# Gate and up products of sixteen experts: the high and low halves of the tokens as one moving operand of 512 columns

## The chip, the core and the metric

The kernel runs on one core of a Trainium2 chip. The time is device microseconds of one execution, from start to end. A profiled execution also leaves a trace: when each instruction ran on TensorE (PE), VectorE (DVE), ScalarE (ACT), GpSimd (POOL) and in the DMA queues, and what ended each idle stretch.

## The reference

One layer: a mixer, and then a mixture of experts that choose their tokens. The change lies in the experts. Each of 16 experts takes the 256 tokens that score highest for it, out of 2048.

```
aff = softmax(h @ w_router + b_router)                 # 2048 x 16
gate, idx = top_k(aff.T, 256)                          # per expert
xe = h[idx]                                            # 16 x 256 x 1024
hid = silu(xe @ w_gate) * (xe @ w_up)                  # 1024 -> 1024, per expert
ye = (hid @ w_down) * gate                             # 1024 -> 1024
out = rms_norm(h_lat + gt2 * scatter_add(idx, ye)) * final_norm_g
```

All of it is fp32. The kernel keeps that precision by splitting every matrix operand into a high part, which TensorE's fp32r format holds, and a low part, the rest. A product is then three matmuls: high by high, high by low and low by high.

## The kernel before

The experts run one after the other, in `moe`. The list below follows one of them, number e.

**Weights.** An expert has six chunks of 1024 x 512: gate and up for the first 512 hidden columns, gate and up for the second 512, and two of the down matrix. They are called gate 0, up 0, gate 1, up 1, down 0 and down 1 here. Each comes in two halves of 256 columns (a and b). For a half, `load_w` issues a DMA of 1 MB into `raw` (2 buffers), ACT casts it to the high part `wh` (L183) and DVE subtracts to get the low part `wl` (L184). That subtraction frees the `raw` buffer for the next DMA. There are three buffers for whole chunks, so a chunk's cast waits until TensorE has finished the chunk three places before it.

**Tokens.** `route(e)` turns the scores into token numbers: 16 compares on DVE (`oh`, L1334), 32 small matmuls (L1339), and a reduction on DVE that writes `idx` (L1343). `idx` has two buffers. `expert_in(e)` then gathers 256 rows of `f_rows` with two indirect DMAs from POOL's queue (`xg`, L1364), turns them with 16 TensorE transposes (`xt`, L1372), and splits them into `xS` (ACT L1374, DVE L1375). For most experts this is done for expert e+1 while expert e is in its first half.

**Gate and up.** Eight tiles of 128 hidden columns, called f0 to f7 here. A tile of `ps_a` (PSUM, three buffers, name `gu`) holds gate and up sums, 2 x 256 tokens. Each is 8 x 3 matmuls of 256 columns by `mm3` (L194 to L196). ACT takes the SiLU out of PSUM (L1392), DVE multiplies with the up half out of PSUM (L1393), and ACT and DVE split the result into `hS` (L1395, L1396).

**Down.** 96 matmuls of 512 columns (`dn`, the same L194 to L196) in four groups; DVE scales each group into `ye` (L1412). When both groups of one half of the tokens are there, POOL issues an indirect DMA that adds 128 rows of `ye` to `h_rows` (L1449). It reads the token numbers in `idx`. The second half's DMA waits for the first half's. The last three experts read the rows and write them back in place of adding, and `final_tile` does the last norm for the rest, beside experts 13 and 14.

**What sets the order.** The instructions of each engine stand in one fixed order, which a scheduler chose when the program was built, by a timeline of its own. It may put instructions of two experts side by side. On each engine they run in that order.

**Buffers that bind.** `idx` of expert e+1 takes the buffer of expert e-1, and so it can only be written when the gathers and the adding DMAs of expert e-1, which read that buffer, have landed. `xS` has one buffer, so the split for e+1 waits for the last gate and up matmul of e.

Of the kernel before, what the change touches and what calls it, by code (L numbers as in the profile page):

```python
# [7 lines left out]
F32 = mybir.dt.float32  # L8
F32R = mybir.dt.float32r
# [3 lines left out]
AF = mybir.ActivationFunctionType  # L13
OP = mybir.AluOpType
AX = mybir.AxisListType
PS = bass.MemoryType.PSUM
DR = bass.MemoryType.DRAM

P = 128
D = 1024  # L20
KT = 8
# [1183 lines left out]
def moe(tc, ctx, env):  # L1205
    nc = tc.nc
# [5 lines left out]
    with ExitStack() as pd:  # L1212
# [2 lines left out]
            raw_f = pf.enter_context(tc.tile_pool(name="rawF", bufs=2, side="right"))  # L1215
            pre = [load_w(raw_f, wr, w[0, 0, :, 0:512], nc.gpsimd, parts=PP, cast=C1) for w in (w_gate, w_up)]
        rt = pd.enter_context(tc.tile_pool(name="rtD", bufs=1))
        ps_a = pd.enter_context(tc.tile_pool(name="psaD", bufs=3, space=PS))
        ps_d = pd.enter_context(tc.tile_pool(name="psdD", bufs=2, space=PS))
        ps_t = pd.enter_context(tc.tile_pool(name="pstD", bufs=2, space=PS))  # L1220
        ps_c = pd.enter_context(tc.tile_pool(name="pscD", bufs=1, space=PS))

        tk = ExitStack()
        wk = tk.enter_context(tc.tile_pool(name="wkT", bufs=1))
        vp = ps_c.tile([P, 2, P], F32, name="c")
        for s in range(2):
            nc.tensor.transpose(vp[:, s, :], AFF[:, s].rearrange("p e g -> p (e g)"), ident)
        blkb, belb, cand, step, cK, siob = topc
# [8 lines left out]
        X = nhi  # L1237
        cd = cand[:, 0, :]
        for i in range(15):
            tp = ps_c.tile([P, 512], F32, name="c")  # L1240
            nc.tensor.matmul(tp[:, 0:3], blkb, cK, start=True, stop=False)
            cn = wk.tile([P, 2], BF, name="cn", bufs=15)
            for j in range(2):
                jk = wk.tile([P, 256], BF, name=f"jk{j}", bufs=1)
                cj = nc.vector.tensor_scalar(jk, X, cd[:, j:j + 1], None, op0=OP.is_le, op1=OP.add,
                                             accum_out=cn[:, j:j + 1])
            if i == VI:
                after_first = cj
            ca = wk.tile([P, 1], BF, name="ca", bufs=15)
            jk = wk.tile([P, 256], BF, name="jk2", bufs=1)  # L1250
            with nc.allow_low_precision(reason="whole numbers up to 256 are exact"):
                nc.scalar.activation(jk, X, AF.Sign, scale=-1.0, bias=cd[:, 2:3], accum_out=ca)
            nc.tensor.matmul(tp[:, 0:2], blkb, cn, start=False, stop=False)
            nc.tensor.matmul(tp[:, 2:3], blkb, ca, start=False, stop=True)
            if i not in (6, 14):
                tcd = wk.tile([P, 4], F32, name="tcd", bufs=15)
                nc.vector.tensor_tensor(tcd, cand[:, i + 1, :], cd[:, 3:4].to_broadcast([P, 4]), op=OP.add)
            if i == 14:
                lob = wk.tile([P, 1], F32, name="lob", bufs=1)
                nc.vector.tensor_scalar(lob, cd[:, 3:4], -1.0, float(LO0), op0=OP.mult, op1=OP.add)  # L1260
            ge = wk.tile([P, 3], F32, name="ge", bufs=15)
            inc = wk.tile([P, 1], F32, name="inc", bufs=15)
            nc.vector.scalar_tensor_tensor(ge, tp[:, 0:3], CAP - 0.5, step[:, i:i + 1].to_broadcast([P, 3]),
                                           op0=OP.is_ge, op1=OP.mult, accum_out=inc)
            if i == 6:
                npre = wk.tile([P, 1], F32, name="npre", bufs=1)
                nc.vector.tensor_tensor(npre, cd[:, 3:4], inc, op=OP.subtract)
                t1 = wk.tile([P, 256], U16, name="t1", bufs=1)
                t2 = wk.tile([P, 256], U16, name="t2", bufs=1)
                nc.vector.scalar_tensor_tensor(t1, nhi, npre, nlow, op0=OP.is_equal, op1=OP.mult)  # L1270
                nc.vector.tensor_scalar(t2, nhi, npre, float(LO0), op0=OP.is_gt, op1=OP.mult)
                nc.vector.tensor_tensor(t1, t1, t2, op=OP.max)
                X = t1
                cd = cand[:, 7, :]
                hb = wk.tile([P, 1], I32, name="hb", bufs=1)
                nc.vector.tensor_scalar(hb, npre, -65536.0, 65536.0 * HI0, op0=OP.mult, op1=OP.add)
            elif i < 14:
                cd = wk.tile([P, 4], F32, name="cd", bufs=15)
                nc.vector.tensor_tensor(cd, tcd, inc.to_broadcast([P, 4]), op=OP.subtract)
# [7 lines left out]
        eq = wk.tile([P, 256], BF, name="eq", bufs=1)  # L1287
        nc.vector.tensor_scalar(gt, V, thr, None, op0=OP.is_gt, op1=OP.add, accum_out=ct[:, 0:1])
        nc.vector.tensor_scalar(eq, V, thr, None, op0=OP.is_equal, op1=OP.add, accum_out=ct[:, 1:2])
        tp = ps_c.tile([P, 512], F32, name="c")  # L1290
        nc.tensor.matmul(tp[:, 0:2], belb, ct, start=True, stop=True)
        nc.tensor.matmul(tp[:, 2:3], blkb, ct[:, 0:1], start=True, stop=True)
        off = wk.tile([P, 3], F32, name="off", bufs=1)
# [11 lines left out]
        nc.vector.scalar_tensor_tensor(se, se, off[:, 1:2], eq, op0=OP.add, op1=OP.mult)  # L1305
        nc.vector.scalar_tensor_tensor(sg, sg, BIG, se, op0=OP.add, op1=OP.add)
        SL = rt.tile([P, 2, NE, 8], F32, name="SL", bufs=1)
        sp = ps_c.tile([P, 2, P], F32, name="c")
        for s in range(2):
            nc.tensor.transpose(sp[:, s, :], sg[:, s * P:(s + 1) * P], ident)  # L1310
        nc.vector.tensor_copy(SL.rearrange("p s e g -> p s (e g)"), sp)
# [16 lines left out]
        wk = pd.enter_context(tc.tile_pool(name="wkD", bufs=1))  # L1328

        def route(e):  # L1330
            oh = ohp.tile([P, 2, 8, 256], BF, name="oh", bufs=1)
            for s in range(2):
                for g in range(8):
                    nc.vector.tensor_scalar(oh[:, s, g, :], siob, SL[:, s, e, g:g + 1], None, op0=OP.is_equal)  # L1334
            rp = ps_c.tile([P, 2, 256], F32, name="c")
            for hf in range(2):
                for i in range(16):
                    s, g = divmod(i, 8)
                    nc.tensor.matmul(rp[:, hf, 0:5], oh[:, s, g, hf * P:(hf + 1) * P], vals[:, s, e, g, :],  # L1339
                                     start=(i == 0), stop=(i == 15))  # L1340
            idx = rt.tile([P, 2], I32, name="idx", bufs=2)
            with nc.allow_low_precision(reason="token numbers are whole"):
                nc.vector.tensor_reduce(idx, rp[:, :, 0:2], axis=AX.X, op=OP.add)  # L1343
            rs = rt.tile([P, 2, 5], F32, name="rs", bufs=2)
            nc.vector.tensor_copy(rs, rp[:, :, 0:5])
            gate = rt.tile([P, 2], F32, name="gate", bufs=2)
            nc.vector.tensor_tensor(gate, rs[:, :, 2], rs[:, :, 3], op=OP.add)
            nc.vector.tensor_tensor(gate, gate, rs[:, :, 4], op=OP.add)
            return idx, gate
# [10 lines left out]
        def expert_in(e):  # L1360
            idx, gate = route(e)
            xg = wk.tile([P, 2, D], F32, name="xg", bufs=1)
            for hf in range(2):
                last[1] = nc.gpsimd.indirect_dma_start(out=xg[:, hf, :], out_offset=None, in_=f_rows,  # L1364
                                                       in_offset=bass.IndirectOffsetOnAxis(ap=idx[:, hf:hf + 1], axis=0))
            xS = [wk.tile([P, KT, 256], F32R, name=f"xS{s}", bufs=1) for s in range(2)]
            for kk in range(4):
                ps = ps_t.tile([P, 2, 256], F32, name="xt")
                for k2 in range(2):
                    for hf in range(2):  # L1370
                        k = 2 * kk + k2
                        nc.tensor.transpose(ps[:, k2, hf * P:(hf + 1) * P], xg[:, hf, k * P:(k + 1) * P], ident)  # L1372
                ks = slice(2 * kk, 2 * kk + 2)
                nc.scalar.activation(xS[0][:, ks, :], ps, AF.Copy)  # L1374
                last[0] = nc.vector.tensor_tensor(xS[1][:, ks, :], ps, xS[0][:, ks, :].bitcast(F32), op=OP.subtract)  # L1375
            return idx, gate, xS

        def expert(e, st, mid=None):
# [3 lines left out]
            for i in range(2):  # L1382
                gw = next_w(w_gate[0, e, :, i * 512:(i + 1) * 512])
                uw = next_w(w_up[0, e, :, i * 512:(i + 1) * 512])
                for f in range(4):
                    fs = slice(f * P, (f + 1) * P)
                    pg = ps_a.tile([P, 2, 256], F32, name="gu")
                    for j, w in enumerate((gw, uw)):
                        for k in range(KT):
                            mm3(pg[:, j, :], w[0][:, k, fs], w[1][:, k, fs], xS[0][:, k, :], xS[1][:, k, :], k, KT)  # L1390
                    sg_ = wk.tile([P, 256], F32, name="sgl", bufs=2)
                    nc.scalar.activation(sg_, pg[:, 0, :], AF.Silu)  # L1392
                    nc.vector.tensor_tensor(sg_, sg_, pg[:, 1, :], op=OP.mult)  # L1393
                    ff = 4 * i + f
                    nc.scalar.activation(hS[0][:, ff, :], sg_, AF.Copy)  # L1395
                    nc.vector.tensor_tensor(hS[1][:, ff, :], sg_, hS[0][:, ff, :].bitcast(F32), op=OP.subtract)  # L1396
                if mid is not None and i == 0:
                    nx = mid()
# [195 lines left out]
```

## Time and profile before

| What | Value |
|---|---|
| Median of 3 runs | 2503.82 us (2495.16 to 2510.73) |
| Profiled execution: its time, its span | 2509.17 us, 2507.4 us |
| PE busy | 2360.6 us, 94% of the span |
| DVE, ACT, POOL busy | 1594.8, 1114.9, 526.2 us |
| Mean granted TensorE clock | 0.968 of full speed |
| DMA moved | 528.97 MB, mean 211 GB/s |

A busy PE is not PE at its peak: the records of its matmuls overlap, so the pace is read from the distance between their starts. The engines other than PE are idle for a good part, and that costs nothing unless somebody waits.

### The profile page before, as it was taken

To read this page: it belongs to the slowest core of one execution; us is meant where nothing else is said; L and a number is where in the kernel's file an instruction comes from. 1 tells how busy PE (TensorE), PEld (TensorE's weight loads), DVE (VectorE), ACT (ScalarE), POOL (GpSimd) and SP (SyncE) were. 2 spreads that over 40 slices of the span, in tenths; PEclk is the share of its full clock that TensorE was granted. 3 is DMA by queue.
4 is the path that set the end of the run, shared out by engine and by line. 5 is a ranking of instruction groups with operands and counts; after the bars stand their busy time and mean duration, and the time that the engine had idled before them with its cause. 6 is when DMAs were issued, how large, how long until landed. Compare 5 with 4: busy or idle time off the path is not lost.

```text
span 2507.4 us, 43163 instructions
## 1 busy us (share of the span) xinstructions
PE 2360.6 (94%) x16841; PEld 2159.0 (86%) x16841; DVE 1594.8 (64%) x3337; ACT 1114.9 (44%) x2002; POOL 526.2 (21%) x420
## 2 busy tenths in 40 slices
PE   7999999998889999999937999999999999999997
PEld 4999999887768898888826999999999999998897
DVE  6688665468778465676674556555565565556674
ACT  4554555576623443343322444444444444444553
POOL 2321222211022633232252011111111011011211
PEclk9999999999988999999967999999999999999999
DMA  8676654499946997565353676666766766668894
GB/s 260 199 231 206 208 171 161 141 298 304 281 128 187 264 274 227 192 197 175 139 168 110 190 230 202 195 200 211 219 212 190 220 210 199 205 208 270 304 309 145
DMA packets 473056, 528.97 MB, mean 211 GB/s; under 512 B 104500, under 2 KB 392061, under 8 KB 470803
## 3 DMA queue, kind: packets, MB, share of 16 engines
q1 hardware_dynamic: 455298, 465.63, 58.3%
q0 software_dynamic: 17120, 59.77, 8.3%
q8 instruction: 133, 2.18, 0.4%
q10 hardware_dynamic: 432, 0.79, 0.1%
q14 instruction: 73, 0.59, 0.1%
HBM read 400.45 MB, written 125.67 MB: 210 GB/s over the span
## 4 chain that ended last, share of the span: by engine, by line
PE 59%; DMA 12%; issue 6%; DVE 5%; ACT 3%; POOL 2%; SPq 0%; POOLq 0%; DVEq 0%; ACTq 0%
PE gu L195 6%; PE gu L196 6%; PE gu L194 6%; DMA xg<-f_rows,idx 4%; PE dn L195 4%; PE dn L194 4%; PE dn L196 4%; PE uv L194 2%; PE uv L196 2%; PE uv L195 2%; PE mx L194 2%; PE mx L196 2%; PE mx L195 2%; ACT wh L183 2%; PE ks L1005 1%
## 5 line engine op out<-in xcount | busy, mean ns | idle before, releaser
L184 DVE TENSOR_TENSOR wl<-raw,wh 128x2048 fp32r<-128x2048 f32 (+1 forms) x212 | 445.8, 2114 | 306.2 <-ACT wh L183 306.1
L194 PE MATMUL gu<-xS,wh 128*128 128x256 f32 x2048 | 580.6, 285 | 3.7 <-ACT wh L183 3.5
L196 PE MATMUL gu<-xS,wl 128*128 128x256 f32 x2048 | 578.6, 285 | 4.8 <-DVE wl L184 4.8
L195 PE MATMUL gu<-xS,wh 128*128 128x256 f32 x2048 | 580.3, 284 | 0.0
L183 ACT ACTIVATE wh<-raw 128x2048 fp32r<-128x2048 f32 (+1 forms) x218 | 381.5, 1771 | 372.2 <-DMA raw<-in_w_gate_dram 146.4
L194 PEld LDWEIGHTS gu<-xS,wh 128*128 128x128 f32 x2048 | 393.5, 192 | 5.9 <-ACT wh L183 4.2
L196 PEld LDWEIGHTS gu<-xS,wl 128*128 128x128 f32 x2048 | 391.8, 192 | 6.8 <-DVE wl L184 5.7
L195 PEld LDWEIGHTS gu<-xS,wh 128*128 128x128 f32 x2048 | 393.6, 192 | 1.1
L194 PE MATMUL pj<-aS,wh 128*128 128x258 f32 x832 | 238.2, 290 | 2.3 <-DVE y L460 2.3
L195 PE MATMUL pj<-aS,wh 128*128 128x258 f32 x832 | 238.3, 288 | 0.2 <-DVE aS L358 0.2
L196 PE MATMUL pj<-aS,wl 128*128 128x258 f32 x832 | 237.6, 287 | 0.6 <-DVE wl L184 0.6
L195 PE MATMUL dn<-wl,hS 128*128 128x512 f32 (+1 forms) x520 | 201.9, 389 | 1.8 <-DVE wl L184 1.8
L194 PE MATMUL dn<-wh,hS 128*128 128x512 f32 (+1 forms) x520 | 203.5, 391 | 0.0
L1449 POOL DMA_INDIRECT h_rows<-ye,idx x26 | 66.5, 2558 | 644.4 <-DVE ye L1412 551.7
L196 PE MATMUL dn<-wh,hS 128*128 128x512 f32 (+1 forms) x520 | 200.9, 387 | 0.0
L194 PEld LDWEIGHTS pj<-aS,wh 128*128 128x128 f32 x832 | 157.1, 190 | 3.6 <-issue 2.0
L195 PEld LDWEIGHTS pj<-aS,wh 128*128 128x128 f32 x832 | 158.6, 191 | 0.6 <-DVE aS L358 0.4
L196 PEld LDWEIGHTS pj<-aS,wl 128*128 128x128 f32 x832 | 157.9, 190 | 1.0 <-DVE wl L184 0.8
L194 PE MATMUL uv<-wh,ast 128*128 128x512 f32 x384 | 155.1, 404 | 0.0
L196 PE MATMUL uv<-wh,ast 128*128 128x512 f32 x384 | 151.7, 395 | 0.0
L195 PE MATMUL uv<-wl,ast 128*128 128x512 f32 x384 | 151.5, 395 | 0.0
L1395 ACT ACTIVATE hS<-sgl 128x256 fp32r<-128x256 f32 x128 | 53.0, 414 | 180.2 <-DVE sgl L1393 180.1
(479 smaller groups left out, 4583.8 us busy)
## 6 DMA issues: line engine op xcount, KB each, us to landing
raw<-in_w_gate_dram SPq DMA_DIRECT2D x64, 1024.0 KB
raw<-in_w_up_dram SPq DMA_DIRECT2D x64, 1024.0 KB
raw<-in_w_down_dram SPq DMA_DIRECT2D x64, 1024.0 KB
kv<-kv SPq DMA_DIRECT2D x140, 256.0 KB
raw<-in_w_mod_dram SPq DMA_DIRECT2D x18, 1024.0 KB
a_sp<-aS SPq DMA_DIRECT2D x32, 512.0 KB
ast<-a_sp POOLq DMA_DIRECT2D x16, 1024.0 KB, 7.6
raw<-in_w_in_dram SPq DMA_DIRECT2D x12, 1024.0 KB
```

Source lines behind the costliest of these rows:

```text
L183: nc.scalar.activation(wh[:, ks, s:s + 256], raw[:, ks], AF.Copy)
L184: (lo_eng or nc.vector).tensor_tensor(wl[:, ks, s:s + 256], raw[:, ks], wh[:, ks, s:s + 256].bitcast(F32), op=OP.subtract)
L194: pace(nc.tensor.matmul(ps, ah, bh, start=(k == 0), stop=False), after)
L195: nc.tensor.matmul(ps, ah, bl, start=False, stop=False)
L196: return nc.tensor.matmul(ps, al, bh, start=False, stop=(k == nk - 1))
L1005: nc.tensor.matmul(sp[:, h, :], kr[:, h, :], vn[:, h, :], start=True, stop=True)
L1395: nc.scalar.activation(hS[0][:, ff, :], sg_, AF.Copy)
L1449: nc.gpsimd.indirect_dma_start(out=h_rows, out_offset=bass.IndirectOffsetOnAxis(ap=idx[:, hf:hf + 1], axis=0), in_=ye[:, hf, :], in_offset ...
```

## The change

- The two parts of the tokens become one tile, `xS[:, 0]` high and `xS[:, 1]` low. One matmul with the high weights streams both, 512 columns, into one PSUM bank of 2 x 256; a second with the low weights streams the high tokens, 256 columns, onto the first half of that bank. So 16 x 8 x 2 x 8 x 3 = 6144 matmuls become 4096, over the same number of columns.
- A `gu` tile grows from one bank to two. `ps_a` goes from three buffers to two, and the separate pool for the routing (`ps_c`, one bank) is gone: routing uses the transposes' pool, under the name `xt`.
- On the way out ACT copies the low halves of gate and up into a new tile `gus` (L1393 now), DVE adds the high halves to it out of PSUM (L1394), and SiLU, product and split go on from `gus` (L1396 to L1400).

```diff
-        ps_a = pd.enter_context(tc.tile_pool(name="psaD", bufs=3, space=PS))
+        ps_a = pd.enter_context(tc.tile_pool(name="psaD", bufs=2, space=PS))
...
-        ps_c = pd.enter_context(tc.tile_pool(name="pscD", bufs=1, space=PS))
+        ps_c = ps_t
...
-            rp = ps_c.tile([P, 2, 256], F32, name="c")
+            rp = ps_c.tile([P, 2, 256], F32, name="xt")
...
-            xS = [wk.tile([P, KT, 256], F32R, name=f"xS{s}", bufs=1) for s in range(2)]
+            xS = wk.tile([P, 2, KT, 256], F32R, name="xS", bufs=1)
...
-                    pg = ps_a.tile([P, 2, 256], F32, name="gu")
+                    pg = ps_a.tile([P, 2, 2, 256], F32, name="gu")
                     for j, w in enumerate((gw, uw)):
                         for k in range(KT):
-                            mm3(pg[:, j, :], w[0][:, k, fs], w[1][:, k, fs], xS[0][:, k, :], xS[1][:, k, :], k, KT)
-                    sg_ = wk.tile([P, 256], F32, name="sgl", bufs=2)
-                    nc.scalar.activation(sg_, pg[:, 0, :], AF.Silu)
-                    nc.vector.tensor_tensor(sg_, sg_, pg[:, 1, :], op=OP.mult)
+                            nc.tensor.matmul(pg[:, j], w[0][:, k, fs], xS[:, :, k, :], start=(k == 0), stop=False)
+                            nc.tensor.matmul(pg[:, j, 0], w[1][:, k, fs], xS[:, 0, k, :], start=False, stop=(k == KT - 1))
+                    gu_ = wk.tile([P, 2, 256], F32, name="gus", bufs=2)
+                    nc.scalar.activation(gu_, pg[:, :, 1, :], AF.Copy)
+                    nc.vector.tensor_tensor(gu_, pg[:, :, 0, :], gu_, op=OP.add)
+                    sg_ = gu_[:, 0, :]
+                    nc.scalar.activation(sg_, sg_, AF.Silu)
+                    nc.vector.tensor_tensor(sg_, sg_, gu_[:, 1, :], op=OP.mult)
```

The scheduler orders all of `moe` anew. The pieces below are from the same place, expert 2 with the routing of expert 3.

DVE before, from the product of f2 to the second half of up 1. `idx` is expert 3's; the waits on DMASW are those for the POOL queue's DMAs that read its buffer.

```order
L1393 TENSOR_TENSOR sgl_16312<-sgl_16312,gu_16263 128x256 [waits Activation_49]
L1396 TENSOR_TENSOR hS1_16134<-sgl_16312,hS0_16133 128x256 [waits Activation_49]
L184 TENSOR_TENSOR wl_16472<-raw_16473,wh_16471 128x8x256 [waits DMAHW4_49,PE_49,Activation_49]
L1343 TENSOR_REDUCE idx_16421<-c_16388 128x2 [waits DMASW6_49,DMASW5_49,DMASW7_49,DMASW4_49,PE_49]
L1345 COPY rs_16423<-c_16388 128x10
L1334 TENSOR_SCALAR oh_17062<-siob_123,SL_14656 128x256 x5
L184 TENSOR_TENSOR wl_16472<-raw_16477,wh_16471 128x8x256 [waits DMAHW5_49,Activation_49]
```

DVE now, from the second half of gate 1 (the first row) to the sum of f1. `gu_15925` is f0, `gu_15965` is f1.

```order
L184 TENSOR_TENSOR wl_16175<-raw_16180,wh_16174 128x8x256 [waits DMAHW3_49,Activation_49]
L1394 TENSOR_TENSOR gus_15958<-gu_15925,gus_15958 128x512 [waits Activation_49]
L1343 TENSOR_REDUCE idx_16135<-xt_16102 128x2 [waits DMASW6_49,DMASW5_49,DMASW7_49,DMASW4_49,PE_49]
L1345 COPY rs_16137<-xt_16102 128x10
L1334 TENSOR_SCALAR oh_16663<-siob_123,SL_14653 128x256
L1394 TENSOR_TENSOR gus_15998<-gu_15965,gus_15998 128x512 [waits Activation_49]
L1334 TENSOR_SCALAR oh_16663<-siob_123,SL_14653 128x256 x10
```

The write of `idx` has moved from the middle of up 1, after f2, to a place between the sums of f0 and f1. On TensorE the last of the routing's small matmuls have moved with it, from the end of f3 to the end of f1, and the first eight transposes from the middle of f5 to the gap between f3 and f4.

ACT before, from the SiLU of f2 to that of f3 (`wh` is up 1, then the first half of down 0):

```order
L1392 ACTIVATE sgl_16312<-gu_16263 128x256
L1395 ACTIVATE hS0_16133<-sgl_16312 128x256
L183 ACTIVATE wh_16471<-raw_16473 128x8x256
L183 ACTIVATE wh_16471<-raw_16477 128x8x256
L1392 ACTIVATE sgl_16366<-gu_16317 128x256
L183 ACTIVATE wh_16698<-raw_16700 128x8x256
```

ACT now, from the copy of f0 to that of f3 (`wh` is up 1):

```order
L1393 ACTIVATE gus_15958<-gu_15925 128x512
L1393 ACTIVATE gus_15998<-gu_15965 128x512
L1396 ACTIVATE gus_15958<-gus_15958 128x256
L1396 ACTIVATE gus_15998<-gus_15998 128x256
L1399 ACTIVATE hS0_15903<-gus_15958 128x256
L1399 ACTIVATE hS0_15903<-gus_15998 128x256
L1393 ACTIVATE gus_16038<-gu_16005 128x512
L1396 ACTIVATE gus_16038<-gus_16038 128x256
L1399 ACTIVATE hS0_15903<-gus_16038 128x256
L183 ACTIVATE wh_16184<-raw_16186 128x8x256
L183 ACTIVATE wh_16184<-raw_16190 128x8x256
L1393 ACTIVATE gus_16078<-gu_16045 128x512
```

The casts of up 1 still stand behind f2, but f2's own way out now stands behind those of f0 and f1, which need DVE's sums.

## Rows read from the trace of the kernel before

**Rows 1.** Busy time by stretch: start:end, us, PE, PEld, DVE, ACT, POOL, PEclk, DMA, GB/s

```profile
1506.28:1577.44 71.16, 70.89 (x530) 66.70 (x529) 42.01 (x56) 30.44 (x32) 9.57 (x4) 1.00 0.67 207
...
2220.29:2507.40 287.11, 266.45 (x1912) 247.63 (x1910) 180.39 (x233) 130.27 (x164) 47.61 (x46) 0.98 0.74 249
```

**Rows 2.** Timeline, PE: start, us, engine, line, operation, idle before

```profile
1582.11 0.28 PE L195 MATMUL gu<-xS,wh 128*128 128x256 f32 x1
1582.23 0.28 PE L196 MATMUL gu<-xS,wl 128*128 128x256 f32 x1
...
1606.91 0.39 PE L195 MATMUL dn<-wl,hS 128*128 128x512 f32 x1
1607.14 0.39 PE L196 MATMUL dn<-wh,hS 128*128 128x512 f32 x1
...
1593.15 0.88 PE L1372 MATMUL xt<-ident,xg 128*128 128x128 f32 x6 [0.95 <-DMA xg<-f_rows,idx]
```

**Rows 3.** PE's waits from 1435 to 2220 us: total, times, longest

```profile
PE xt L1372 <- DMA xg<-f_rows,idx: 5.4, 9, 1.0
```

**Rows 4.** Groups by line, 1577.4 to 1649.2 us: busy us, mean ns of one

```profile
L1393 DVE TENSOR_TENSOR sgl<-sgl,gu 128x256 f32<-128x256 f32 x8 | 3.3, 417 | 6.3 <-ACT sgl L1392 6.3
...
L1375 DVE TENSOR_TENSOR xS<-xt,xS 128x512 fp32r<-128x512 f32 x4 | 2.6, 682 | 0.0
...
L1374 ACT ACTIVATE xS<-xt 128x512 fp32r<-128x512 f32 x4 | 2.1, 585 | 0.0
```

**Rows 5.** Timeline, ACT: down 1 of experts 2 and 3, expert 4's up 0, gate 1

```profile
1531.34 3.72 ACT L183 ACTIVATE wh<-raw 128x2048 fp32r<-128x2048 f32 x2 [1.41 <-PE gu L195]
...
1603.18 3.72 ACT L183 ACTIVATE wh<-raw 128x2048 fp32r<-128x2048 f32 x2 [1.41 <-PE gu L195]
...
1625.19 1.92 ACT L183 ACTIVATE wh<-raw 128x2048 fp32r<-128x2048 f32 x1 [0.96 <-DMA raw<-in_w_up_dram]
...
1635.37 1.92 ACT L183 ACTIVATE wh<-raw 128x2048 fp32r<-128x2048 f32 x1 [1.67 <-DMA raw<-in_w_gate_dram]
```

**Rows 6.** Timeline, DVE: `idx` of expert 4, compares, then expert 3's third `ye`

```profile
1581.60 0.15 DVE L1343 TENSOR_REDUCE idx<-c 128x2 int32<-128x4 f32 x1
...
1581.74 1.06 DVE L1334 TENSOR_SCALAR oh<-siob,SL 128x256 bf16<-128x256 bf16 x5
...
1626.47 0.74 DVE L1412 SCALAR_TENSOR_TENSOR ye<-dn,gate,gt2r 128x512 f32<-128x512 f32 x1
1627.14 2.29 DVE L184 TENSOR_TENSOR wl<-raw,wh 128x2048 fp32r<-128x2048 f32 x1
```

**Rows 7.** Timeline, POOL: the adding DMAs of experts 3 and 4

```profile
1627.50 3.43 POOL L1449 DMA_INDIRECT h_rows<-ye,idx  x1 [41.65 <-DVE ye L1412]
1638.63 2.44 POOL L1449 DMA_INDIRECT h_rows<-ye,idx  x1 [7.70 <-DMA h_rows<-ye,idx]
...
1699.96 1.62 POOL L1449 DMA_INDIRECT h_rows<-ye,idx  x1 [42.30 <-DVE ye L1412]
1707.55 2.56 POOL L1449 DMA_INDIRECT h_rows<-ye,idx  x1 [5.96 <-DMA h_rows<-ye,idx]
```

**Rows 8.** Chain of waits, expert 12: start, us, what; then `h_rows`' DMAs

```profile
2277.34 10.30 DMA h_rows<-ye,idx
...
DMA to landing us min/median/max: 5.7/9.3/10.8
```

**Rows 9.** Chain of waits: experts 0's and 4's gather; casts behind TensorE

```profile
1333.36 5.49 DMA xg<-f_rows,idx
1435.07 1.92 ACT wh L183
...
1583.39 9.71 DMA xg<-f_rows,idx
...
2220.29 1.92 ACT wh L183
```

**Rows 10.** Busy time in a stretch of expert 13, columns as in rows 1

```profile
2300.00:2304.00 4.00, 2.53 (x15) 2.33 (x14) 4.00 (x9) 2.35 (x3) 1.64 (x2) 0.77 0.73 195
```

More of the change, by code (lines that the diff above doesn't have):

```diff
@@ L1217, in moe @@
         rt = pd.enter_context(tc.tile_pool(name="rtD", bufs=1))
-        ps_a = pd.enter_context(tc.tile_pool(name="psaD", bufs=3, space=PS))
+        ps_a = pd.enter_context(tc.tile_pool(name="psaD", bufs=2, space=PS))
         ps_d = pd.enter_context(tc.tile_pool(name="psdD", bufs=2, space=PS))
         ps_t = pd.enter_context(tc.tile_pool(name="pstD", bufs=2, space=PS))
-        ps_c = pd.enter_context(tc.tile_pool(name="pscD", bufs=1, space=PS))
+        ps_c = ps_t
         tk = ExitStack()
         wk = tk.enter_context(tc.tile_pool(name="wkT", bufs=1))
-        vp = ps_c.tile([P, 2, P], F32, name="c")
+        vp = ps_c.tile([P, 2, P], F32, name="xt")
         for s in range(2):
@@ L1239, in moe @@
         for i in range(15):
-            tp = ps_c.tile([P, 512], F32, name="c")
+            tp = ps_c.tile([P, 512], F32, name="xt")
             nc.tensor.matmul(tp[:, 0:3], blkb, cK, start=True, stop=False)
@@ L1289, in moe @@
         nc.vector.tensor_scalar(eq, V, thr, None, op0=OP.is_equal, op1=OP.add, accum_out=ct[:, 1:2])
-        tp = ps_c.tile([P, 512], F32, name="c")
+        tp = ps_c.tile([P, 512], F32, name="xt")
         nc.tensor.matmul(tp[:, 0:2], belb, ct, start=True, stop=True)
@@ L1307, in moe @@
         SL = rt.tile([P, 2, NE, 8], F32, name="SL", bufs=1)
-        sp = ps_c.tile([P, 2, P], F32, name="c")
+        sp = ps_c.tile([P, 2, P], F32, name="xt")
         for s in range(2):
@@ L1373, in expert_in @@
                 ks = slice(2 * kk, 2 * kk + 2)
-                nc.scalar.activation(xS[0][:, ks, :], ps, AF.Copy)
-                last[0] = nc.vector.tensor_tensor(xS[1][:, ks, :], ps, xS[0][:, ks, :].bitcast(F32), op=OP.subtract)
+                nc.scalar.activation(xS[:, 0, ks, :], ps, AF.Copy)
+                last[0] = nc.vector.tensor_tensor(xS[:, 1, ks, :], ps, xS[:, 0, ks, :].bitcast(F32), op=OP.subtract)
             return idx, gate, xS
```

## The prediction

> **What bounds the kernel now.** The busy time by stretch comes first: in the middle of the experts TensorE is busy for 70.9 of 71 us at full clock [rows 1]. From one cast of up 1 to the same cast eleven experts later, both released by TensorE, are 785.2 us: 71.38 us an expert [rows 9]. TensorE's starts give the pace: 0.120 us for a matmul of 256 columns, 0.23 for 512 [rows 2] (0.227 over a longer run of the down product's starts). So 384 gate and up matmuls take 46.1 us, 96 down matmuls 21.8, 16 transposes 1.8, the routing 0.8: 70.5. The rest, 0.9, is the wait for the gathered tokens [rows 2, 3], the only one that the list of TensorE's waits has in eleven experts. From expert 13 on it is otherwise: 287 us with 20 of them idle and DMA at 249 GB/s, not 207 [rows 1]. There the weights and the last norm's traffic set the pace.
>
> I then read who will be late if TensorE runs faster, on three timelines. All times below are from Z, the start of an expert's first cast of down 1 (1603.18 for expert 3) [rows 5]. That cast follows the gate half of f7, so Z returns once per expert. Up 0's second half is cast at Z+22.0, gate 1's at Z+32.2 [rows 5]. The third `ye` is done at Z+24.0 [rows 6], the first adding DMA is issued at Z+24.3 and the second at Z+35.5, when the first has landed [rows 7]. The second lands some 10 us on [rows 8]: Z+46. The `idx` for the expert after next, which needs exactly that landing, is written at 1581.60 [rows 6], 50.3 us after the Z of expert 2 at 1531.34 [rows 5]. It does not wait there: some 4 us are to spare.
>
> **What the change removes.** Per expert, 128 triples of 3 x 0.120 become pairs of 0.227 + 0.120 [rows 2]: 0.013 us each, 1.7 us. A column costs the same; what goes is a fixed price per matmul, 0.120 less 256 columns at 2.4 GHz (0.107). The Trainium skill, "TensorE: Matmul & The Clock Gate", section "Wait — 56ns, not 53.3ns?", gives that fixed price as about 2.5 ns; by it the change would give back 2048 x 2.5 ns, 5 us in the whole kernel and not 27. The trace's rows say 13 ns, and the sum goes by them. That the two runs of 256 columns lie 8 KB apart is not in any row; between no price and the whole 1.7 us I take none, as nearest to the contiguous row.
>
> **What it adds.** ACT copies 128x512 out of PSUM, DVE adds 128x512: 0.585 and 0.682 us by the same shapes [rows 4], eight times each, 10 us on engines that are busy for 30 and 42 of 71 us [rows 1]. By themselves they cost nothing. The place of three things in the order does cost.
>
> *f0's sum.* ACT copies f0 only after both casts of gate 1 (Z+34.1); DVE subtracts until Z+36.4 and adds until Z+37.1. TensorE has the rest of f7, 92 down matmuls, 8 transposes, f0, f1 and routing before f2: 2.8 + 20.9 + 0.9 + 11.1 + 0.8 = 36.5. With two buffers f2 needs f0's. Price 0.6 us, up to 4 where gate 1 comes late. TensorE runs f2 from Z+37.1.
>
> *`idx`, next on DVE.* It now stands between the sums of f0 and f1, at Z+37.1, and still needs the landing of the previous expert's adding DMAs. These do not come sooner: DVE now does both subtractions of up 0 before the third `ye`. The cast at Z+22.0 [rows 5], 1.9 for it, 2.3 to subtract and 0.7 for `ye` make Z+27.0, so the first DMA is issued at Z+27.3 and not Z+24.3. From first to second it is 11.1 or 7.6 us (8 of the 13 pairs of that timeline lie near the first, mean 9.9) [rows 7], to the landing 9.3 in the middle, 10.3 for expert 12 [rows 8]. Landing: Z+46.4, between Z+43 and Z+49. Until then DVE waits, and everything behind `idx` with it. That is f1's sum, the products and low halves of f0 and f1, f2's sum and the subtraction of up 1.
>
> *Who waits for that.* Let L be the landing.
> - f3 needs f1's buffer. After `idx`, a copy and one compare DVE adds f1 until L+1.2. TensorE ended f2 at Z+42.7; it starts f3 at Z+47.6, 4.9 us late, and ends it at L+6.8.
> - The gather follows `idx`. From `idx` to the second gather's issue 1.8 us (1581.60 to 1583.39 [rows 6, 9]), then 5.5 in a quiet queue or 9.7 beside weights [rows 9]. Weights are not loading then, so L+7.3, and f4 starts after the transposes at L+8.3.
> - ACT casts up 1 after f2 has left, which needs f2's copy, after f1's `hS`, after f0's and f1's products, after 15 compares of 0.21 (1.06 for five [rows 6]). I add L+1.2, 2.1 for the first ten, 2.4 for the rest up to the low half of f0, then 0.6 copy, 0.7 sum [rows 4], 0.4 each for SiLU, product and `hS` (the product's row [rows 4] for all three) and a few hand-overs: the cast starts at L+8.3. With 1.9 [rows 5] and 2.3 [rows 6] the low half is there at L+12.5. f4's up half needs it; its gate half ends at L+11.1. So 1.3 us, and f4 ends at L+15.1.
> - Down 0's load starts only then and takes as long as gate 1's last one, from the subtraction before to its cast, 1629.4 to 1635.4 at most [rows 5, 6], 5.1 taken. Its cast ends at L+19.6, and f4's copy stands behind the cast, its sum behind the subtraction: L+22.6. f6 needs that buffer at L+21.6. With f3's sum behind up 1 (0.5) that is 1.5 us more.
> - f6, a few down matmuls and f7's gate half: next Z at L+31.4.
>
> So an expert takes 46.4 + 31.4 = 77.8 us in place of 71.4: 6.4 more, with the 1.7 us already taken off. From L = 43 to 49 it is 3 to 9. TensorE at rest for some 5 us can also lose its clock: a stretch of 4 us in expert 13 with 1.5 us of rest has a granted clock of 0.77 [rows 10], so half of it was at 1.2 GHz. A few us at that level would cost some 2 us of f3, most of which the later waits take in; I leave it to the top of the range.
>
> The SBUF page of the Trainium skill ("SBUF — State Buffer", under "SBUF: two separate sides") says that a DVE operation on two ports keeps GpSimd from writing the descriptors of its DMAs. POOL's rows do show one issue of the same kind at 3.43 and one at 1.62 us [rows 7]. If that is why, a DVE at rest lets the second DMA go sooner: L less by 1 to 2 us, and 12 to 24 us less in all.
>
> **The sum.** Twelve whole experts (Z of expert 0 to Z of expert 12) by 6.4 are 77 us. Expert 13 waits once more on the same DMA, but it also waited before, for the norm's rows behind it: 3. `idx` of expert 15 waits for the last rows of expert 13: 3. Expert 0 gains 2. Together +81 on the profiled 2509, that is 2590, and by the same ratio on the median of 2503.8: 2585 us. Range of this case alone: 3 an expert gives 2540, 9 with 12 in the tail gives 2621; with the clock 2635.
>
> **Rivals.**
> 1. *Faster: the adding DMA lands before DVE asks.* If L is under Z+37, DVE never waits, the gather comes before f3 ends (its 0.9 us goes) and an expert is 71.4 - 1.7 - 0.9 + 0.6 for f0 and some 0.3 for tokens split late = 69.7. Thirteen of them give -22: 2482 us. For it: the first pair of DMAs came 7.6 us apart, and the smallest landing is 5.7 [rows 7, 8]; 27.3 + 7.5 + 5.7 = 40.5. Against it: even that is past 37. It would need the third `ye` earlier than I have it. The point from which L decides is Z+40: there L + 31.4 is the old 71.4. 0.08.
> 2. *Same: L near Z+40.* The block is there, and the 2.6 us taken off pay for it. 2490 to 2525. For it: fast pairs, and a POOL that writes unhindered. Against it: eight of thirteen pairs are slow. 0.12.
> 3. *Worse: the clock as well.* If each wait of 5 us halves the clock for a few us and nothing takes that in, 3 us an expert come on top, and with the late landings that is 2640 and more. Against it: by the steps above, the gather and up 1 come later than a slow f3 ends. 0.05.
> 4. *The wide matmul does not run at 0.227.* Then 1.7 x 16 = 27 us more, inside the range.
>
> **How the numbers follow.** The forecast holds 0.75, the rivals 0.08, 0.12 and 0.05. A measurement of this kernel tells about 1% from no change, 25 us. Faster by that: rival 1 in most cases, 0.06. Same: the rest of it and rival 2, 0.12. Slower: 0.82. The range is 2500 to 2630. It leaves out rival 1, the low part of 2, and 3 with the top of the forecast: 0.19.
>
> **What the changed profile would show.** If I am right: DVE's longest waits are at `idx`, for the DMA into `h_rows`, 6 to 12 us each in thirteen experts; TensorE waits at f3 for the sum of f1 and is about 10% idle between experts 1 and 12; casts of up 1 are 77 to 79 us apart; and the gate and up pairs start 0.35 us apart. If `idx` begins without a wait, the whole sum is wrong and rival 1 holds. If DVE waits but casts are less than 74 us apart, L is what I have wrong. If TensorE's waits name the weights and not PSUM, the new sums disturb the weight stream in a way that I did not follow.

## The result and the profile after

| | Before | After |
|---|---|---|
| Median of 4 runs | 2505.09 us (2495.16 to 2510.73) | 2597.59 us (2595.02 to 2600.49) |
| Ratio, 95% interval | | 1.0378 (1.0346 to 1.0411) |
| Span of the profiled execution | 2507.4 us | 2598.7 us |
| PE busy, share of the span | 94% | 91% |

The kernel is slower by 92.5 us; 2585 was forecast, in a range of 2500 to 2630. All times below are of one expert unless said otherwise, and Z is the start of its first cast of down 1, as in the prediction.

The timeline of ACT gives Z for expert 0, for expert 2, for expert 3 and for expert 12. The third row is the cast of up 1, the fourth that of the second half of down 0.

```profile
1390.79 1.91 ACT L183 ACTIVATE wh<-raw 128x2048 fp32r<-128x2048 f32 x1 [1.85 <-PE gu L1390]
...
1551.17 3.72 ACT L183 ACTIVATE wh<-raw 128x2048 fp32r<-128x2048 f32 x2 [0.40 <-PE gu L1390]
...
1605.26 3.70 ACT L183 ACTIVATE wh<-raw 128x2048 fp32r<-128x2048 f32 x2
...
1617.60 1.91 ACT L183 ACTIVATE wh<-raw 128x2048 fp32r<-128x2048 f32 x1 [0.54 <-DMA raw<-in_w_down_dram]
...
1629.11 3.72 ACT L183 ACTIVATE wh<-raw 128x2048 fp32r<-128x2048 f32 x2 [0.38 <-PE gu L1390]
...
2325.17 3.72 ACT L183 ACTIVATE wh<-raw 128x2048 fp32r<-128x2048 f32 x2 [0.38 <-PE gu L1390]
```

Twelve experts take 934.4 us: 77.87 each, where it was 71.38 [rows 9]. That is 77.8 us of the 91.3 by which the span grew. The timeline of DVE shows where an expert stops: `idx` between the sums of f0 and f1, with a wait that [rows 6] do not have.

```profile
1588.57 0.68 DVE L1394 TENSOR_TENSOR gus<-gu,gus 128x512 f32<-128x512 f32 x1
1597.46 0.16 DVE L1343 TENSOR_REDUCE idx<-xt 128x2 int32<-128x4 f32 x1 [8.21 <-issue]
...
1597.81 0.69 DVE L1394 TENSOR_TENSOR gus<-gu,gus 128x512 f32<-128x512 f32 x1
```

POOL at the same time, to be read beside [rows 7]: the two adding DMAs of expert 2, and the gather that follows `idx`.

```profile
1578.56 1.62 POOL L1453 DMA_INDIRECT h_rows<-ye,idx  x1 [56.39 <-DVE ye L1416]
1587.57 2.55 POOL L1453 DMA_INDIRECT h_rows<-ye,idx  x1 [7.38 <-DMA h_rows<-ye,idx]
1597.89 1.00 POOL L1364 DMA_INDIRECT xg<-f_rows,idx  x1 [7.78 <-DVE oh L1334]
```

And PE, from the last matmul of f2 to the first of f3, and the wait for down 0:

```profile
1594.95 0.28 PE L1391 MATMUL gu<-xS,wl 128*128 128x256 f32 x1
1598.55 0.50 PE L1390 MATMUL gu<-xS,wh 128*128 128x512 f32 x1 [3.32 <-DVE gus L1394]
...
1619.57 0.73 PE L194 MATMUL dn<-wh,hS 128*128 128x512 f32 x2 [1.25 <-ACT wh L183]
```

The profile does not name the DMA as what ended DVE's wait. It puts 8 of the 13 waits down to "issue" and 5 to a matmul (59.7 and 30.3 us, 90.0 together). The distance names it: `idx` begins 9.89 us after the second adding DMA was issued, and 9.0 to 11.3 us after it in twelve of thirteen experts. For six of these DMAs the trace has the landing too, 8.8 to 11.1 us after the issue, and `idx` begins 0.2 us behind it each time. The proof is the first experiment.

PE's waits from 1435 to 2220 us, where [rows 3] had only the gather (total, times, longest):

```profile
PE gu L1390 <- DVE gus L1394: 30.7, 21, 4.0
PE dn L194 <- ACT wh L183: 16.8, 10, 3.5
```

Busy time by stretch, columns as in [rows 1]: the whole expert, and the start of f3.

```profile
1551.17:1629.11 77.94, 72.52 (x402) 60.81 (x401) 47.02 (x65) 35.38 (x41) 6.13 (x4) 0.98 0.61 189
1598.50:1602.00 3.50, 3.45 (x12) 2.91 (x13) 3.50 (x18) 1.02 (x3) 1.36 (x2) 0.58 0.62 181
```

After that wait of 3.3 us the granted clock is 0.58 for 3.5 us: TensorE runs mostly at 1.2 GHz there. In [rows 10] it was 0.77.

### The profile page after: what moved, and what is told of

Its sections match the earlier page's. It is cut to its first block, busy times and chain, and to the rows that moved or that the text cites. A ratio compares the mean times of both kernels' runs of the same rounds, so it can differ in the third digit from the quotient of the medians.

```text
span 2598.7 us, 39328 instructions
## 1 busy us (share of the span) xinstructions
PE 2377.0 (91%) x14793; PEld 2057.3 (79%) x14793; DVE 1674.7 (64%) x3465; ACT 1191.4 (46%) x2130; POOL 502.6 (19%) x420
## 4 chain that ended last, share of the span: by engine, by line
PE 34%; DMA 22%; DVE 14%; issue 8%; ACT 7%; POOL 2%; SPq 1%; POOLq 0%; DVEq 0%; ACTq 0%
PE gu L1390 5%; ACT wh L183 5%; DVE wl L184 5%; DMA h_rows<-ye,idx 5%; DMA raw<-in_w_gate_dram 3%; DMA raw<-in_w_up_dram 3%; DMA raw<-in_w_down_dram 3%; PE gu L1391 3%; PE mx L194 2%; PE mx L196 2%; DMA GB<-gn 2%; PE mx L195 2%; DVE oh L1334 1%; PE ks L1005 1%; PE pj L194 1%
## 5 line engine op out<-in xcount | busy, mean ns | idle before, releaser
L1390 PE MATMUL gu<-xS,wh 128*128 128x512 f32 x2048 | 755.6, 409 | 54.2 <-DVE gus L1394 42.4
L1390 PEld LDWEIGHTS gu<-xS,wh 128*128 128x128 f32 x2048 | 394.6, 193 | 157.2 <-DVE gus L1394 51.1
L1391 PEld LDWEIGHTS gu<-xS,wl 128*128 128x128 f32 x2048 | 398.0, 194 | 19.5 <-DVE wl L184 16.7
L1453 POOL DMA_INDIRECT h_rows<-ye,idx x26 | 53.6, 2061 | 831.8 <-DVE ye L1416 750.0
L1396 ACT ACTIVATE gus<-gus 128x256 f32<-128x256 f32 x128 | 53.2, 417 | 225.3 <-DVE gus L1394 224.9
L194 PEld LDWEIGHTS dn<-wh,hS 128*128 128x128 f32 x520 | 96.9, 188 | 44.0 <-ACT wh L183 23.3
L1394 DVE TENSOR_TENSOR gus<-gu,gus 128x512 f32<-128x512 f32 x128 | 87.7, 686 | 46.0 <-ACT gus L1393 45.7
```

Source lines behind the costliest of these rows:

```text
L194: pace(nc.tensor.matmul(ps, ah, bh, start=(k == 0), stop=False), after)
L1390: nc.tensor.matmul(pg[:, j], w[0][:, k, fs], xS[:, :, k, :], start=(k == 0), stop=False)
L1391: nc.tensor.matmul(pg[:, j, 0], w[1][:, k, fs], xS[:, 0, k, :], start=False, stop=(k == KT - 1))
L1394: nc.vector.tensor_tensor(gu_, pg[:, :, 0, :], gu_, op=OP.add)
L1396: nc.scalar.activation(sg_, sg_, AF.Silu)
L1453: nc.gpsimd.indirect_dma_start(out=h_rows, out_offset=bass.IndirectOffsetOnAxis(ap=idx[:, hf:hf + 1], axis=0), in_=ye[:, hf, :], in_offset ...
```

## The experiments

Each starts from the changed kernel ("after") or the kernel before, as its diff says. Ratios are to the kernel before, on the same chip.

**A third buffer for `idx`** (after). It removes the need for the adding DMAs to land, not the wait alone.

```diff
-            idx = rt.tile([P, 2], I32, name="idx", bufs=2)
+            idx = rt.tile([P, 2], I32, name="idx", bufs=3)
```

> The changed kernel with a third buffer for idx; the order of every engine stays the same up to expert 14, so only the wait for the previous expert's adding DMAs goes. Theory A (the whole loss is VectorE's queue held at idx by those DMAs): idx is written without a wait near Z+37, no core of the loss is left, an expert takes 69.5 to 70.5 us, time 2475 to 2500 us. Rival B (the copies, the sums and only two PSUM buffers for gu are what slows TensorE, and idx waits beside it): TensorE goes on waiting for the sums, 2560 us or more. Rival C (half and half): 2510 to 2550.

2517.48 us, ratio 1.0048 (1.003 to 1.0066), where the change alone has 1.0378: some 80 of the 92.5 us are gone. DVE's timeline in the same place: `idx` is at Z+38.3 and waits for nothing.

```profile
1633.46 0.69 DVE L1394 TENSOR_TENSOR gus<-gu,gus 128x512 f32<-128x512 f32 x1
1634.06 0.15 DVE L1343 TENSOR_REDUCE idx<-xt 128x2 int32<-128x4 f32 x1
...
1634.39 0.69 DVE L1394 TENSOR_TENSOR gus<-gu,gus 128x512 f32<-128x512 f32 x1
```

Z of experts 0, 3 and 12, and PE's waits from 1435 to 2220 us (total, times, longest):

```profile
1381.28 1.92 ACT L183 ACTIVATE wh<-raw 128x2048 fp32r<-128x2048 f32 x1 [1.81 <-PE gu L1390]
...
1595.77 3.72 ACT L183 ACTIVATE wh<-raw 128x2048 fp32r<-128x2048 f32 x2 [0.38 <-PE gu L1390]
...
2240.28 3.72 ACT L183 ACTIVATE wh<-raw 128x2048 fp32r<-128x2048 f32 x2 [0.38 <-PE gu L1390]
```

```profile
PE gu L1390 <- DVE xS L1375: 5.7, 11, 1.0
PE gu L1390 <- DVE gus L1394: 5.1, 11, 0.5
PE dn L194 <- ACT wh L183: 2.8, 4, 1.3
```

An expert takes 71.58 us, about as long as before the change (71.38). Theory A names the cause of most of the loss, but the gain it promised (69.5 to 70.5) is not there, and the time misses its range: 2517 lies in that of rival C, "half and half", though far more than half is gone. Of what is left, 7 us lie behind the Z of expert 12 (268.9 us to the end, for 261.8 before).

**The PSUM pools alone** (before: two `gu` buffers of one bank, routing in the transposes' pool), and the same with three `idx` buffers.

```diff
-        ps_a = pd.enter_context(tc.tile_pool(name="psaD", bufs=3, space=PS))
+        ps_a = pd.enter_context(tc.tile_pool(name="psaD", bufs=2, space=PS))
...
-        ps_c = pd.enter_context(tc.tile_pool(name="pscD", bufs=1, space=PS))
+        ps_c = ps_t
```

> The kernel before with the change's PSUM pools alone (two gu buffers of one bank, routing in the transposes' pool); three matmuls of 256 columns, no copy, no sum. The build now puts idx between the product and the split of f1. Theory A: idx waits 5 to 8 us for the adding DMAs in each of 12 experts; f2's product and the cast of up 1 stand behind it, so TensorE waits 2 to 4 us at f4, 72.5 to 76 us an expert: 2520 to 2560 us. Rival B (the loss belongs to the copies and sums): no such wait, or one that costs nothing, 2490 to 2515 us.

> The run with the PSUM pools alone, with a third buffer for idx; the order of VectorE is the same row by row. Theory A: no wait at idx, and the gather comes early enough, so TensorE's wait of 0.9 us for tokens goes: 70.5 us an expert, 2485 to 2500 us. It also prices the wide matmul, against the changed kernel with three idx buffers: with 13 ns a matmul saved (the rows before) that one is 10 to 25 us faster than this; with the 2.5 ns of the Trainium skill's page on TensorE the two are within 5 us. Rival B: 2500 to 2515, and the wide one with three idx buffers far above it.

2538.90 (1.0143, 1.0118 to 1.0169) and 2530.98 (1.0113, 1.0088 to 1.0138). `idx` waited in six experts, five times 1.1 to 2.3 us and once 7.9, and freeing it gave 8 us. The first time lies in A's range, but the waits at `idx` that A named are mostly not there. The rest is PE's. With three buffers, from 1435 to 2220 us:

```profile
PE gu L194 <- DVE sgl L1393: 16.3, 8, 3.5
PE xt L1372 <- DMA xg<-f_rows,idx: 7.0, 6, 2.3
```

So neither theory had it. In every second expert, and more shortly in some others, the SiLU of f0 stands behind a cast of gate 1 whose weights come late. With three `idx` buffers the wide version is 13.5 us faster than this one, but their orders differ, so that is no price of the wide matmul.

**Each half of that** (before): two `gu` buffers alone, routing moved alone, and as a control the third `idx` buffer alone.

```diff
-ps_a = ... bufs=3      # two_gu_buffers
+ps_a = ... bufs=2
...
-ps_c = ... bufs=1      # routing_in_xt
+ps_c = ps_t
...
-idx = ... bufs=2       # before_idx3
+idx = ... bufs=3
```

> The kernel before with two gu buffers in place of three; routing keeps its own bank, idx stays behind f2 and the first half of up 1. Theory A2 (the 24 us that the two PSUM pools cost without any wait at idx come from two gu buffers): 2520 to 2540 us, with TensorE waiting for products. Rival E (they come from the routing in the transposes' pool): 2500 to 2512 us.

> The kernel before with the routing in the transposes' PSUM pool and three gu buffers. Theory A2: 2500 to 2512 us, no change. Rival E: 2520 to 2540 us, with TensorE waiting at transposes or at the routing's matmuls.

> The kernel before with a third idx buffer and nothing else; the order of VectorE is the same row by row. Every theory: idx did not wait there, so 2495 to 2515 us, no change. If it is over 1% faster, idx waited before as well, unseen, and the change alone did not bring the wait.

Routing: 2505.14, ratio 0.9999 (0.9972 to 1.0026), no change. Control: 2502.59, 0.9993 (0.9975 to 1.0011), no change. Two buffers: 2537.96, 1.0138 (1.0116 to 1.016), as A2 expected, but not for its reason. The new order has `idx` early in every second expert, and it waits there, seven times 8.1 to 9.6 us. DVE's row, then PE's:

```profile
1573.36 0.16 DVE L1343 TENSOR_REDUCE idx<-c 128x2 int32<-128x4 f32 x1 [8.50 <-issue]
```

```profile
1573.42 0.28 PE L196 MATMUL gu<-xS,wl 128*128 128x256 f32 x1
1576.79 0.39 PE L194 MATMUL gu<-xS,wh 128*128 128x256 f32 x1 [3.09 <-DVE sgl L1393]
```

The stretch before and the stretch after that wait:

```profile
1565.00:1573.40 8.40, 8.40 (x72) 8.40 (x71) 0.04 (x1) 2.49 (x3) 0.99 (x1) 1.00 0.75 193
...
1576.80:1581.40 4.60, 4.60 (x27) 4.60 (x28) 1.18 (x3) 1.55 (x4) 1.04 (x2) 0.66 0.91 315
```

The clock again: 0.66 in the 4.6 us after it.

**Two `gu` buffers and three `idx` buffers** (before): the first and the third of these edits together.

> The run with two gu buffers, with a third buffer for idx; the build puts idx of every second expert still earlier, before the third ye, where a free buffer lets it go at once. In the run with two gu buffers VectorE stood at idx for 8 us in every second expert, before the products of f0's neighbour and the second half of gate 1. Theory A3 (its 33 us are this wait, not the two buffers): 2500 to 2515 us, no wait at idx. Theory A2 (they are the two buffers): 2525 us or more, with TensorE still waiting for products.

2499.21, ratio 0.9973 (0.996 to 0.9985): A3. PE's only wait from 1435 to 2220 us:

```profile
PE gu L194 <- DVE sgl L1393: 0.6, 1, 0.6
```

Two buffers cost nothing by themselves in this order. It is the fastest version of all, though not by a per cent. The build moved `idx` as well, so the pair is not as clean as the others.

**`idx` held behind f2** (after). `f2[0]` is the split of f2.

```diff
-                nc.vector.tensor_reduce(idx, rp[:, :, 0:2], axis=AX.X, op=OP.add)
+                with tc.issue_after(f2[0].ins) if f2 else ExitStack():
+                    nc.vector.tensor_reduce(idx, rp[:, :, 0:2], axis=AX.X, op=OP.add)
```

> The changed kernel with idx held behind the split of f2 on VectorE, as it stood before; two idx buffers. Nothing of the products stands behind the wait but the subtraction of up 1. The build moves the first transposes to the middle of f4. Theory A: idx waits 0 to 2 us (it comes at Z+46), f3 starts on time, TensorE waits up to 3.5 us for the gather in f4 instead: 70 to 73.5 us an expert, 2490 to 2535 us. Rival B: waits for the sums remain, 2560 us or more.

2571.38, 1.0257 (1.0224 to 1.029), which misses A's range and lies in that of rival B. `idx` at Z+47.7 no longer waits, but PE does (the edit shifts the line numbers):

```profile
PE xt L1374 <- DMA xg<-f_rows,idx: 24.3, 12, 3.1
PE gu L1392 <- DVE gus L1396: 14.2, 10, 1.4
```

An expert takes 75.1 us. Waits for the sums remain, as B said, but the larger part is another: the late `idx` makes the gather late, 2.0 us at each of 12 waits for its tokens. The place of `idx` has a price on both sides.

**f0's copy ahead of the second cast of gate 1** (after), with two and with three `idx` buffers; the order is the same up to expert 13. `hold` is f0's copy while gate 1 is loaded, `s` the half.

```diff
-                    nc.scalar.activation(wh[:, ks, s:s + 256], raw[:, ks], AF.Copy)
+                    with tc.issue_after(hold[0].ins) if hold and s else ExitStack():
+                        nc.scalar.activation(wh[:, ks, s:s + 256], raw[:, ks], AF.Copy)
```

> The changed kernel, two idx buffers, with the second cast of gate 1 held behind the copy of f0 on ACT. The build's order now has idx early (behind the product of f0, before the sum of f1) in every second expert only, seven in all, and behind f2 in the others. Theory A (each early idx waits some 6 to 8 us for the adding DMAs and costs its expert 6 to 7 us): seven blocked experts at 77 to 78 us, the others near 71: 2530 to 2560 us, half of the loss of the changed kernel. Rival B (the copies and sums slow every expert): all experts alike, 2575 us or more.

> The same with three idx buffers; the order is the same row by row up to expert 13. Theory A: the seven waits go, and with f0's copy one cast earlier TensorE's wait of 0.9 us at f2 goes as well: 70 to 71.2 us an expert, 2488 to 2512 us. Rival F (what is left with three idx buffers is the later weight stream, which this delays by another cast): 2515 to 2530 us.

2557.37 (1.0207, 1.0182 to 1.0232) and 2517.69 (1.0055, 1.0034 to 1.0076). The first time lies in A's range, the second in that of rival F. The seven early `idx` waited 4.9 to 8.2 us, and taking these waits away gave 39.7 us. The 11 us that the third buffer alone had left stayed (13 here): PE's waits with three buffers are other ones than in that run, of the same 1.3 us an expert. That the later weight stream is what is left, as F says, is not shown.

```profile
PE gu L1396 <- DVE gus L1400: 4.9, 7, 1.2
PE gu L1397 <- DVE wl L187: 3.3, 5, 0.7
PE gu L1396 <- DVE xS L1378: 2.8, 6, 0.5
```

**More room in PSUM** (after, three `idx` buffers): gate and up in one-bank tiles of their own, four buffers; and three `gu` tiles of two banks, with one bank for `dn` and one for `xt`.

```diff
-                    pg = ps_a.tile([P, 2, 2, 256], F32, name="gu")
                     for j, w in enumerate((gw, uw)):
+                        pg = ps_a.tile([P, 2, 256], F32, name="gu")
...
-ps_a, ps_d, ps_t = 2, 2, 2 buffers     # three_wide_buffers
+ps_a, ps_d, ps_t = 3, 1, 1 buffers
```

> The changed kernel with three idx buffers, and with gate and up sums in PSUM tiles of their own (one bank each, four buffers in place of two of two banks), copied and added one by one. With three idx buffers alone 2517 us were left, 71.6 us an expert, with TensorE waiting some 1.3 us for f0's sum and the low half of the tokens. Theory A2 (what is left of the loss is two buffers that come free late): a bank comes free while the other half still runs, so TensorE's waits for the sums go, 70 to 71 us an expert: 2490 to 2508 us. Rival D (what is left is ACT's and VectorE's longer way out of PSUM, more instructions on both): 2515 to 2530 us, or more, since this has twice as many copies and sums.

> The changed kernel with three idx buffers and three gu tiles of two banks; one bank is left for the down groups and one for transposes and routing together. Theory: what is left of the loss with three idx buffers is TensorE's wait of 0.9 us at f2 for f0's sum, and 0.6 for the low half of the tokens; the third buffer takes the first of them away, and down groups are covered, since gate and up matmuls of the next expert lie between them: 70 to 71 us an expert, 2480 to 2505 us. Rival: the single banks bring waits of their own, for the scaling into ye (0.75 us a group) and for the copies of the transposes: 2515 us or more.

2582.87 (1.032, 1.0294 to 1.0346) and 2624.84 (1.0476, 1.0448 to 1.0503). The theory missed in both, and `idx` waited for no DMA. The rivals had only a lower bound, 2515 us or more, and both times lie above it; but of the waits that they named only those for the copies of the transposes are found to any amount, 8.3 us with three tiles. The build ordered everything anew, and PE waits mostly for weights, tokens and `hS` (half tiles, then three tiles):

```profile
PE xt L1372 <- DMA xg<-f_rows,idx: 14.0, 5, 3.5
PE gu L1391 <- ACT wh L183: 13.9, 10, 2.9
```

```profile
PE gu L1390 <- ACT wh L183: 16.6, 11, 2.1
PE dn L194 <- ACT hS L1399: 11.4, 10, 2.2
PE gu L1391 <- DVE wl L184: 11.3, 10, 1.3
PE xt L1372 <- DVE xS L1375: 8.3, 10, 1.0
```

Of buffers alone they say nothing, since the order changed with them.

## Why the prediction was right

**The cause.** Three pairs with long waits differ in the third `idx` buffer: the changed kernel, 13 waits and 80.1 us; f0's copy first, 7 waits and 39.7 us; two `gu` buffers, 7 waits and 38.8 us (some 41 by the ratios, since these two ran on different chips). That is 6.2, 5.7 and 5.5 us a wait (the first two with the same order up to expert 13). In a fourth pair, the PSUM pools alone with the same order throughout, six waits of mostly 1 to 2 us gave 8 us. Where `idx` never waited, in the kernel before, the buffer gave 2 us, within the noise. So `idx` ahead of f1's sum, held by the adding DMA, is shown to be most of the loss, 80 of the 92.5 us. What the other 12 are is not shown in full.

**The steps.** L is the landing of the second adding DMA, read here as the start of `idx`, for experts 0 to 11.

| Step | Forecast | Measured |
|---|---|---|
| First adding DMA issued | Z+27.3 | Z+27.0 to 28.4 |
| f0's sum ends | Z+37.1 | Z+38.0 to 39.0 |
| L | Z+46.4, between 43 and 49 | Z+44.0 to 47.1, mean 45.4 |
| f3 starts | L+1.2 | L+1.1 to 1.3 |
| Cast of up 1 | L+8.3 | L+7.8 |
| Last cast of down 0 ends | L+19.6 | L+22.0 to 24.2 |
| Next Z | L+31.4 | L+31.5 to 31.7 in nine of twelve, 34.4 to 35.3 in three |
| An expert | 77.8 us | 77.87 us |

L came early because the second DMA went 7.3 to 9.0 us after the first and not 9.9. Behind down 0 PE waits for the cast, not for f4's buffer as I had it.

That the mean of an expert fits so well is partly luck: L is 1.0 short, the way from L to Z 1.1 long. The make-up was off as well. From the Z of expert 1 to that of expert 12 TensorE is idle for 6.6% of the time (busy 795.65 of 852.18 us), where the prediction named about 10%. It is busy for 72.3 us an expert, 70.9 before, where the prediction took 1.7 off; the mean granted clock is 0.98 there and was 1.00. Of the other signs, the waits at `idx` came (6.0 to 8.9 us in twelve experts, 3.4 in the thirteenth), and the pairs 0.35 us apart; casts of up 1 are 75.6 to 82.2 us apart and not 77 to 79.

**What was off by a size.** The sum was +81 for the profiled execution, and +91.3 came. The twelve experts gave +77.8 (forecast 77). Expert 0 lost 2 where I had it gain 2, and from the Z of expert 12 to the end it is 273.5 us, for 261.8: +11.7 and not +6. In that tail PE waits 9.0 us for sums of `gu`, with the norm's work on ACT and DVE beside them; I had counted `idx` alone there. Of its two terms the first came, a wait of 3.4 us, but `idx` of expert 15 did not wait.

**The clock** was a rival of 0.05, and half of it came. In the six experts with L at 44 f3 waits 1.1 to 1.3 us and the clock stays; in the six with L past 46 it waits 3.2 to 4.0, and the clock falls for some 3 to 6 us. Forecast was that later waits take that in. They do in four of those six: from L to the next Z it is 31.5 to 31.7 us, as in the experts where the clock stays. In three experts, two of them with such a fall, PE waits once more, 2.5 to 3.5 us for down 0, and in the 4 us behind that wait the clock is 0.57 to 0.65.

**What was removed** was mis-sized. 1.7 us an expert went by 0.227 for the wide matmul, with no price for its two runs 8 KB apart. The starts of one gate and up tile, first and fifteenth pair after it:

```profile
1695.88 0.39 PE L1390 MATMUL gu<-xS,wh 128*128 128x512 f32 x1
...
1701.17 0.40 PE L1390 MATMUL gu<-xS,wh 128*128 128x512 f32 x1
```

5.29 us for 15 pairs, 0.353 each (0.351 over 119 pairs), for three at 0.120: 0.9 to 1.2 us an expert. So rival 1 (2482 us without the block) was too fast by some 35 us. In the run without the block, with three `idx` buffers, the gate and up matmuls take 1.5 us an expert less than in the kernel before. But the down product takes 0.7 more (last section), and the waits are 1.3 us for 0.5; the two take back all of it. (These are sums of the distances between starts in eleven experts, with the idle time taken off.) The 0.9 us of waiting for tokens, which the prediction let go in rival 1, was misread: [rows 3] have 5.4 us in eleven experts, 0.5 each.

Whether the saving is a fixed price per matmul, the runs do not settle. With two `idx` buffers a pair takes 9 ns less than three matmuls of the kernel before, 0.351 for 0.360, nearer to the 13 of [rows 2]. With three buffers it is 3 ns, 0.347 for 0.350. That is near the 2.5 ns that the Trainium skill gives ("TensorE: Matmul & The Clock Gate", section "Wait — 56ns, not 53.3ns?"), by which 128 matmuls less would be an estimated 0.3 us an expert.

**POOL beside a subtraction.** The prediction left room for L to come 1 to 2 us sooner, should a subtraction on DVE hold up POOL's write of a DMA, as the Trainium skill's "SBUF — State Buffer" would have it of a DVE operation on two ports (under "SBUF: two separate sides"). The traces agree. In the kernel before, eight of the thirteen first issues begin while a subtraction runs and take 3.3 to 3.5 us; the other five take 1.6. In the changed kernel no subtraction runs beside the first issue, and all thirteen take 1.6. Each second issue begins during one and ends 1.5 us after it. Here it ends at 1588.66, and the issue at 1587.57 + 2.55 = 1590.12:

```profile
1584.16 4.50 DVE L184 TENSOR_TENSOR wl<-raw,wh 128x2048 fp32r<-128x2048 f32 x2 [1.25 <-ACT wh L183]
```

In all fourteen traces these two cases give the length of an issue, with three exceptions in 364. That the first issue is never held up fits an L that is 1.0 early.

**Left open.** No version was found in which the wide operand gains anything.

## What to carry to other kernels

A change to buffers or to the shape of a tile is also a change to the order, if a scheduler sets it. Look in the new order for writes that overwrite what a DMA in flight still reads: on an engine that runs in order, such a write holds everything behind it, and a small buffer more may be all that it needs. Price a saving per instruction by the stage as a whole; here, without the block, 1.5 us of gate and up matmuls were met by 0.8 us more of waits and a down product slower by 0.7 us.

## What the runs showed of the hardware that I had not expected

**TensorE's pace moves by some 2.5%, up or down, with a third `idx` buffer.** In the kernel before, a matmul of the down product starts every 0.2278 us and one of 256 columns every 0.1199 (means of 94 and 366 starts in one expert). With three `idx` buffers and the same order of every engine it is 0.2334 and 0.1168, at a granted clock of 1.00 in both. First the down product of the kernel before, two starts that are 39 matmuls apart:

```profile
1605.98 0.40 PE L194 MATMUL dn<-wh,hS 128*128 128x512 f32 x1
...
1614.85 0.39 PE L194 MATMUL dn<-wh,hS 128*128 128x512 f32 x1
```

Then the run with three buffers, ten matmuls of 256 columns apart, and 39 of 512 apart:

```profile
1604.64 0.28 PE L194 MATMUL gu<-xS,wh 128*128 128x256 f32 x1
...
1605.81 0.28 PE L195 MATMUL gu<-xS,wh 128*128 128x256 f32 x1
...
1606.05 0.39 PE L194 MATMUL dn<-wh,hS 128*128 128x512 f32 x1
...
1615.14 0.40 PE L194 MATMUL dn<-wh,hS 128*128 128x512 f32 x1
```

All seven runs with three `idx` buffers have a down product at 0.2330 to 0.2334, all seven without at 0.2273 to 0.2286. The wide matmul goes the other way, 0.229 with and 0.233 to 0.236 without. What the buffer changes in the built program is that `xS`, `hS` and the tiles between and behind them lie 32 bytes further on in SBUF (`xS` at 163680, not 163648), while the weights stay. That the address is the cause was not tried by itself. If only `xS` were so moved, and it is the cause, the kernel before would by these numbers save an estimated 384 x 0.0031 = 1.2 us an expert, as much as the wide operand saves here with two `idx` buffers.
